# Laying all operands of one-pass matrix products at one residue modulo 512 bytes in a hybrid decoder layer

## The chip, the core and the metric

The kernel runs on one core of one Trainium2 chip. The metric is the device time of one launch in microseconds (us); three runs of the kernel before took 1207.21, 1209.97 and 1210.71 us, median 1209.97 us. Five engines work side by side: TensorE (PE in the rows; its weight loads are PEld), VectorE (DVE), ScalarE (ACT), GpSimd (POOL) and SyncE (SP, which here only issues transfers).

## What is computed

One decoder layer over 512 tokens of 1024 features, in float32. A mixing sublayer projects the normed input once into all branches, runs four of them, and merges them under gates; a gated MLP follows.

```python
def mixing_sublayer(h, mem_n, w_in, ...):
    z = h @ w_in
    xa, ga, q, k, v, us, xq, gates = jnp.split(z, SPLIT_IDX, axis=-1)
    ya = rg_lru_branch(xa, ga, ...)
    yb = dilated_attention(q, k, v)
    yc = s5_branch(us, ...)
    yx = memory_cross_attention(xq, mem_n, mem_wkv)
    g = jax.nn.sigmoid(gates.reshape(B_, L, N_BRANCH, D_MODEL))
    m = (g[:, :, 0] * (ya @ proj_a) + g[:, :, 1] * (yb @ proj_b)
         + g[:, :, 2] * (yc @ proj_c) + g[:, :, 3] * (yx @ proj_x))
    return m @ w_out

def conv_gated_mlp(h, w_up, conv_w, conv_b, w_down):
    up = h @ w_up
    val = up[..., :D_FF]
    gate = causal_dwconv(up[..., D_FF:], conv_w, conv_b)
    return (val * jax.nn.gelu(gate)) @ w_down

def reference(x, mem, ...):
    h = rms_norm(x, g_mix_pre); mem_n = rms_norm(mem, g_mem)
    x = x + rms_norm(mixing_sublayer(h, mem_n, ...), g_mix_post)
    h = rms_norm(x, g_mlp_pre)
    return x + rms_norm(conv_gated_mlp(h, ...), g_mlp_post)
```

## The kernel before

**Products.** A float32 product is made of three one-pass products. Each operand is split into a high part, rounded to the type `float32r` of one pass, and a low part, the rest: `split` (line 94) and `wload` (line 75) do it with a copy on ACT and a subtraction on DVE. Then low·high, high·high and high·low are summed in PSUM; `mm3` (line 83) is the loop for a stored unit of weights. In each product one operand is loaded into the array first (the stationary one, 128 columns of 4 bytes, which are 512 bytes of a partition) and the other streams past it (the moving one, 512 or 256 columns of 4 bytes). In a row such as `up<-h2l,whi` the moving operand stands first and the stationary one second: the activations `h2l` move past the weights `whi`, while in `dn<-whi,aTh` and `wo<-woh,mm0h` the weights move past the activations.

**Weights.** A unit of weights is [128, 1024] float32 (512 KB). `wfetch` (line 70) brings it in on SP's queue, three buffers deep, and `wload` splits it into `whi` and `wlo`, three buffers each. One unit is enough for 24 products of 512 columns.

**Order of the work.** Python writes the instructions in order, and each engine runs its own in that order. The stages are: norms and the memory's keys and values; RG-LRU; memory cross-attention; S5 with the gates of two branches between its steps; dilated attention, twice two heads of each group, with the GLU of S5 and the third branch's gates between; the gates and products with `yb` (`merge(1, yb, 2, ...)`, lines 667 and 669); `w_out` with the residual and the norm (lines 680 to 795); the upward products of the MLP (`up`, line 775, and `upu`, line 808), whose results go through the convolution and GELU on ACT and DVE and are split into `aT` (line 829); the downward products (`down`, line 833); and the last norm.

**Places in SBUF.** Tiles come from pools that lie one behind another, and one side of the memory is filled from the right. The size of each tile fixes the place of the next, so a tile's distance from a multiple of 512 bytes is left to what lies before it. In the built program the weights `whi` and `wlo`, the normed input `hT`, the memory's `mT`, and the branch results `ya`, `yx`, `yc` and the GLU's input `gy`, the merged `mm0` and `mm1`, and `woh` and `wol` all lie at 384 modulo 512; the other operands of one-pass products lie elsewhere (the table in the section on the change).

**Lines that the change touches.** Line 181 (`vx`, the memory's values, in the pool on the right before `xq`), line 451 (`sel0`, a table of 2x128 numbers that is copied to `selr` and used by `combine`, line 596), line 479 (`nmc`, the negated maxima of the attention's rows), line 679 (`cols`, sums of squares, between `h2` and the next tiles of the pool on the right), line 788 (`we`, the fourth unit of upward weights), and line 803 (`fcb`, a bias of the convolution, ahead of `aT`).

The loops that the steps speak of:

```python
def up(b, w, cs, ks=range(KC)):                      # line 775
    for k in ks:
        sl = slice(k * 128, (k + 1) * 128)
        for n, (a, x) in enumerate(((w[0], h2[1]), (w[0], h2[0]), (w[1], h2[0]))):
            PE.matmul(b[:, cs], a[:, sl], x[:, k, cs], ...)

def down(t, nh, k, w):                               # line 833
    for n, (a, b) in enumerate(((0, w[1]), (0, w[0]), (1, w[0]))):
        PE.matmul(acc[t, nh], aT[a][:, k, ts_], b[:, cs], ...)
```

Of the kernel before, what the change touches and what calls it, by code (L numbers as in the profile page):

```python
# [12 lines left out]
F32 = mybir.dt.float32  # L13
F32R = mybir.dt.float32r
# [4 lines left out]
PSUM = bass.MemoryType.PSUM  # L19
# [31 lines left out]
def _body(ctx, tc, nc, D):  # L51
# [31 lines left out]
    def mm3(out, w, x, nk):  # L83
        """out[128, N] = sum over nk chunks of w_k^T x_k, operands given as exact hi + lo parts."""
        whi, wlo = w
        n = 0
        for k in range(nk):
            sl = slice(k * 128, (k + 1) * 128)
            for a, b in ((whi, 1), (whi, 0), (wlo, 0)):
                last = PE.matmul(out, a[:, sl], x[b][:, k], start=(n == 0), stop=(n == 3 * nk - 1))  # L90
                n += 1
        return last

    def split(hi, lo, src, scale=None, eng=V):
        """hi + lo = src (* scale), hi rounded to the width of one pass."""
        if scale is None:
            a = S.copy(hi, src)
            b = eng.tensor_tensor(out=lo, in0=src, in1=f32(hi), op=ALU.subtract)  # L98
        else:
            a = S.activation(hi, src, AF.Identity, scale=scale)  # L100
            b = V.scalar_tensor_tensor(out=lo, in0=src, scalar=scale, in1=f32(hi), op0=ALU.mult, op1=ALU.subtract)
        return a, b
# [11 lines left out]
    def rstd_of(pool, s0, s1, n, tag, bufs=1, between=None, eng=V):  # L114
        """((s0 + s1) / DM + EPS) ** -0.5, with a Newton step after the table's root; between() goes beside the root."""
        t, y, e, r = (pool.tile([128, n], F32, tag=tag + x, name=tag + x, bufs=bufs) for x in "tyer")
        if s1 is None:
            eng.tensor_scalar(out=t, in0=s0, scalar1=EPS * DM, scalar2=None, op0=ALU.add)
        else:
            eng.tensor_scalar(out=t, in0=s0, scalar1=s1, scalar2=EPS * DM, op0=ALU.add, op1=ALU.add)  # L120
        S.activation(y, t, AF.Sqrt, scale=1.0 / DM)
        if between is not None:
            between()
        V.reciprocal(y, y)
        if n == 1:
            eng.tensor_scalar(out=e, in0=y, scalar1=y, scalar2=t, op0=ALU.mult, op1=ALU.mult)
        else:
            eng.tensor_tensor(out=e, in0=y, in1=y, op=ALU.mult)
            eng.tensor_tensor(out=e, in0=e, in1=t, op=ALU.mult)
        eng.tensor_scalar(out=e, in0=e, scalar1=-0.5 / DM, scalar2=1.5, op0=ALU.mult, op1=ALU.add)  # L130
        eng.tensor_tensor(out=r, in0=y, in1=e, op=ALU.mult)
        return r
# [28 lines left out]
    def turned_rows(xs, gain, dst, k0, k1):  # L161
        """dst[k] (hi, lo) <- xs turned to have features on partitions, times gain."""
        for k in range(k0, k1):
            b = axb("nT")
            for t in range(4):
                PE.transpose(b[:, t * 128:(t + 1) * 128], xs[t][:, k * 128:(k + 1) * 128], ident)
            last = split(dst[0][:, k, :], dst[1][:, k, :], b, scale=gain[:, k:k + 1])
        return last

    mp = ctx.enter_context(pool("mp"))  # L170
    # the memory's keys of a head's whole chunks (0 .. 3) and, with the other head's rows at zero, shared ones (4 .. 7)
# [9 lines left out]
    vx = tuple(kvp.tile([128, 2, 768], F32R, name="vx" + s) for s in "hl")  # L181
# [13 lines left out]
    with pool("np") as npool:  # L195
# [9 lines left out]
        # the rows' scale comes after the products  # L205
# [80 lines left out]
    ya = ynew("ya")  # L286
    with pool("lru", bufs=2) as lp, pool("lruc") as lc:
# [5 lines left out]
        with tc.issue_after(normed[0].ins), tc.issue_after(normed[1].ins):  # L293
            for b in (ba, bx):
                V.tensor_scalar(out=b, in0=b, scalar1=0.5, scalar2=None, op0=ALU.mult)
            # softplus(-lam) = max(-lam, 0) + log1p(e), e = exp(-|lam|), by the series of 2 atanh(e / (2 + e))
            V.scalar_tensor_tensor(out=ab, in0=lam, scalar=-1.0, in1=lam, op0=ALU.mult, op1=ALU.max)
            S.activation(e, ab, AF.Exp, scale=-1.0)
            V.tensor_scalar(out=s, in0=e, scalar1=2.0, scalar2=None, op0=ALU.add)
            V.reciprocal(s, s)  # L300
            V.tensor_tensor(out=s, in0=s, in1=e, op=ALU.mult)
            V.tensor_tensor(out=s2, in0=s, in1=s, op=ALU.mult)
            V.memset(q, 1.0 / 17)
            for d in (15, 13, 11, 9, 7, 5, 3, 1):
                V.tensor_tensor(out=q, in0=q, in1=s2, op=ALU.mult)
                V.tensor_scalar(out=q, in0=q, scalar1=1.0 / d, scalar2=None, op0=ALU.add)
            V.tensor_tensor(out=q, in0=q, in1=s, op=ALU.mult)
            V.tensor_scalar(out=ab, in0=lam, scalar1=-1.0, scalar2=0.0, op0=ALU.mult, op1=ALU.max)
            V.scalar_tensor_tensor(out=q, in0=q, scalar=2.0, in1=ab, op0=ALU.mult, op1=ALU.add)
            V.tensor_scalar(out=chf, in0=q, scalar1=4.0, scalar2=None, op0=ALU.mult)  # L310
            V.tensor_scalar(out=nch, in0=q, scalar1=-4.0, scalar2=None, op0=ALU.mult)
# [137 lines left out]
    apx = ExitStack()  # L449
    ap = apx.enter_context(pool("at"))  # L450
    sel0 = ap.tile([2, 128], F32, name="selh")
# [4 lines left out]
    # order of the tokens in a group: 4 tiles of 128  # L456
# [12 lines left out]
    class Attention:  # L469
        """Two heads of each group."""  # L470

        def __init__(self, h2):
            self.h2 = h2
            self.ab = []
            for g, w in enumerate((256, 128, 128)):
                t = ap.tile([128, 2, w], F32, tag="ab%d" % g, name="ab%d" % g)
                nc.gpsimd.dma_start(out=t, in_=D["ab%d" % g][:, 2 * h2:2 * h2 + 2, :])
                self.ab.append(t)
            self.nmc = ap.tile([128, 3, 4, 2], F32, tag="nmc", name="nmc")
            # maxima in columns 0 and 1, sums in 32 and 33  # L480
            self.col = ap.tile([128, 3, 4, 34], F32, tag="col", name="col")
            G.memset(self.col, 0.0)
            self.mcol, self.lcol = self.col[:, :, :, 0:2], self.col[:, :, :, 32:34]
            self.q, self.k, self.v, self.o, self.segs, self.vT = {}, {}, {}, {}, {}, {}
# [16 lines left out]
        def units_k(self, g):  # L501
            b = unit(U_K + 2 * g + self.h2, "k")
            # each head's keys, the other head's rows at zero
# [63 lines left out]
        def weigh(self):  # L567
            # weights of the groups, per head and token: exp(m_g - M) / sum_g exp(m_g - M) l_g
# [40 lines left out]
        def run(self, fill, before=None):  # L609
            """The group's steps between products that don't wait for them; before() comes with the first."""  # L610
# [68 lines left out]
    cols = x1p.tile([128, 16], F32, name="cols")  # L679
    with pool("wo") as wo:  # L680
# [93 lines left out]
        # the first products of the MLP in halves of the tokens, the first of which are there sooner  # L774
# [13 lines left out]
        w = tuple(x1p.tile([128, 1024], F32R, name="we" + s) for s in "hl")  # L788
# [14 lines left out]
    fcb = fp.tile([128, 24], F32, name="fcb")  # L803
# [40 lines left out]
    # the last products by tiles of tokens, whose weights stand where h2 did  # L844
# [32 lines left out]
def s5_params(nc, tc, D, keep_pool, pool):  # L877
    V, S = nc.vector, nc.scalar
    r = {}
    with pool("s5t") as tp:  # L880
# [29 lines left out]
        def exp(o, x):  # L910
            """exp(x) = 2^n exp(r): the power of two from the table, rid of its error by its mantissa's bits, times a polynomial."""
# [31 lines left out]
        # z = (A - 1) / lambda  # L943
# [26 lines left out]
        # powers of A  # L970
# [8 lines left out]
        # a chunk's decay, and the powers 0 .. 15 and 0, 16 .. 112 of its rotation  # L979
# [25 lines left out]
class S5:  # L1005
    """S5 in batches of eight groups (four pairs) over 128 chunks of 4 tokens: lanes are (group of the pair, state)."""
# [12 lines left out]
    def tables(self, i):  # L1019
        """The rotations R^c of the chunks, and V_j = A^(3 - j) B."""  # L1020
# [33 lines left out]
    def prepare(self, i):  # L1054
        """The batch's matrices: inputs to chunk sums, states to outputs, inputs to outputs within a chunk."""
# [7 lines left out]
        # inputs: [(j, group of the pair, h), pair, chunk]  # L1063
# [3 lines left out]
        # W_n = C A^n  # L1067
# [14 lines left out]
        # K_tau = Re(C A^tau B), tau = 0 .. 3, with D on its first diagonal  # L1082
# [55 lines left out]
    def states(self, i):  # L1138
        """The batch's states before each chunk."""
# [7 lines left out]
        # sums of a chunk's inputs, turned back by its rotation  # L1147
# [19 lines left out]
        # states before each chunk  # L1167
# [12 lines left out]
    def outputs(self, i):  # L1180
        """GELU of the batch's outputs, chunks on partitions."""
        S, PE, st = self.nc.scalar, self.nc.tensor, self.b[i]
        U, (xr, xi) = st["U"], st["x"]
        # y: [chunk, pair, (group, j, h)]
# [9 lines left out]
    def turned(self, i):  # L1194
        """The same with features on partitions, tokens in (j, c) order, in a bank of PSUM."""
# [70 lines left out]
```

## Time and profile before

| | |
|---|---|
| three runs | 1207.21, 1209.97, 1210.71 us |
| median | 1209.97 us |
| profiled execution | span of the one core 1209.4 us (first to last instruction); no other time of it is on record |
| PE | 1181.5 us busy, 98% of the span, 5778 products |
| PEld | 970.7 us |
| DVE | 685.4 us |
| ACT | 516.8 us |
| POOL | 132.4 us |
| moved by DMA | 119.16 MB, mean 99 GB/s |

The span is the time from the first to the last instruction on the core; the median of the runs is 0.6 us longer. Products are pipelined: each row of a product lasts some 390 ns from its start to its modelled end, and the next one starts long before that end. So the pace of TensorE is not read from the mean of one product but from a stretch of the chain: its length divided by the number of products in it. The chain is the sequence of work that ended last, followed back from the last instruction.

### The profile page before, as it was taken

What the parts mean: (1) busy time and instruction counts of PE and PEld (TensorE: products, weight loads), DVE (VectorE), ACT (ScalarE), POOL (GpSimd) and SP (SyncE); (2) the same over time, 40 slices, a digit from 0 to 9 for tenths busy, and PEclk for the clock granted to TensorE, in tenths of its full rate; (3) what the DMA queues carried; (4) which work ended last, traced back from release to release, by engine and by line L of the source; (5) the groups of instructions that cost most, each with busy time, mean ns of one, the idle gap of its engine ahead of it and who ended that gap; (6) DMA issues with size and microseconds to landing.
All of it is one profiled execution on the core that took longest, in us unless ns stands there. A gap on an engine that the chain in (4) does not pass through costs nothing.

```text
span 1209.4 us, 15139 instructions
## 1 busy us (share of the span) xinstructions
PE 1181.5 (98%) x5778; PEld 970.7 (80%) x5778; DVE 685.4 (57%) x1246; ACT 516.8 (43%) x871; POOL 132.4 (11%) x172
## 2 busy tenths in 40 slices
PE   7999999999999999999999999999999999999997
PEld 7877788877787887878888888888888888888886
DVE  5756795688797634485447455475445444432224
ACT  5669833553334235443533233455343443421122
POOL 3200100096561000000000000010000000000000
PEclk9999999999999999999999999999999999999999
DMA  6432252122323322213122324613322223223221
GB/s 244 166 105 70 92 180 76 31 83 78 92 76 100 112 90 66 84 62 122 62 79 75 92 92 134 236 37 105 104 89 91 102 87 103 90 89 102 88 87 69
DMA packets 43720, 119.16 MB, mean 99 GB/s; under 512 B 9566, under 2 KB 13744, under 8 KB 43648
## 3 DMA queue, kind: packets, MB, share of 16 engines
q1 hardware_dynamic: 42000, 114.69, 28.6%
q0 software_dynamic: 1072, 2.46, 0.7%
q8 instruction: 45, 0.74, 0.2%
q10 hardware_dynamic: 576, 1.05, 0.2%
q14 instruction: 27, 0.22, 0.1%
HBM read 114.17 MB, written 4.01 MB: 98 GB/s over the span
## 4 chain that ended last, share of the span: by engine, by line
PE 82%; DVE 9%; ACT 4%; DMA 2%; POOL 1%; issue 1%; SPq 0%; DVEq 0%; ACTq 0%; POOLq 0%
PE up L779 22%; PE gate L90 13%; PE dn L837 11%; PE prj L90 7%; PE v L90 3%; PE k L90 3%; PE q L90 3%; PE us L90 3%; PE xq L90 3%; PE glu L90 2%; PE ga L90 2%; DVE wlo L80 1%; PE kv L90 1%; PE kv L257 1%; PE xs L378 1%
## 5 line engine op out<-in xcount | busy, mean ns | idle before, releaser
L80 DVE TENSOR_TENSOR wlo<-wraw,whi 128x1024 fp32r<-128x1024 f32 (+1 forms) x198 | 230.5, 1166 | 290.4 <-ACT whi L79 282.0
L79 ACT CAST whi<-wraw 128x1024 fp32r<-128x1024 f32 (+1 forms) x198 | 194.3, 984 | 455.3 <-PE up L779 110.7
L779 PE MATMUL up<-h2l,whi 128*128 128x512 f32 (+1 forms) x400 | 152.7, 382 | 1.0 <-DVE h2l L98 1.0
L779 PE MATMUL up<-h2h,whi 128*128 128x512 f32 (+1 forms) x400 | 152.6, 381 | 0.0
L779 PE MATMUL up<-h2h,wlo 128*128 128x512 f32 (+1 forms) x400 | 152.5, 381 | 0.0
L90 PE MATMUL gate<-hTl,whi 128*128 128x512 f32 x256 | 101.2, 395 | 0.0
L90 PE MATMUL gate<-hTh,whi 128*128 128x512 f32 x256 | 100.2, 392 | 0.0
L90 PE MATMUL gate<-hTh,wlo 128*128 128x512 f32 x256 | 100.0, 391 | 0.0
L779 PEld LDWEIGHTS up<-h2l,whi 128*128 128x128 f32 x400 | 75.1, 188 | 17.6 <-DVE h2l L98 1.5
L779 PEld LDWEIGHTS up<-h2h,whi 128*128 128x128 f32 x400 | 75.1, 188 | 16.2
L779 PEld LDWEIGHTS up<-h2h,wlo 128*128 128x128 f32 x400 | 75.1, 188 | 16.0
L837 PE MATMUL dn<-whi,aTh 128*128 128x512 f32 x160 | 63.2, 395 | 0.0
L837 PE MATMUL dn<-whi,aTl 128*128 128x512 f32 x160 | 63.2, 395 | 0.0
L837 PE MATMUL dn<-wlo,aTh 128*128 128x512 f32 x160 | 63.2, 395 | 0.0
L90 PEld LDWEIGHTS gate<-hTl,whi 128*128 128x128 f32 x256 | 48.1, 188 | 10.1 <-issue 0.5
L90 PEld LDWEIGHTS gate<-hTh,wlo 128*128 128x128 f32 x256 | 48.1, 188 | 10.0 <-DVE wlo L80 0.2
L90 PEld LDWEIGHTS gate<-hTh,whi 128*128 128x128 f32 x256 | 48.1, 188 | 9.5
L828 DVE TENSOR_TENSOR fc<-fc,up 128x512 f32<-128x512 f32 x24 | 16.5, 689 | 44.8 <-PE up L779 43.5
L825 DVE SCALAR_TENSOR_TENSOR fc<-gs,fcw,fc 128x512 f32<-128x512 f32 x48 | 36.1, 751 | 0.8
L837 PEld LDWEIGHTS dn<-wlo,aTh 128*128 128x128 f32 x160 | 30.0, 188 | 7.3
L837 PEld LDWEIGHTS dn<-whi,aTh 128*128 128x128 f32 x160 | 30.0, 188 | 7.3
L837 PEld LDWEIGHTS dn<-whi,aTl 128*128 128x128 f32 x160 | 30.0, 188 | 7.3
(520 smaller groups left out, 2566.3 us busy)
## 6 DMA issues: line engine op xcount, KB each, us to landing
wraw<-w_in SPq DMA_DIRECT2D x74, 512.0 KB, 3.5
wraw<-ffn_w_up SPq DMA_DIRECT2D x48, 512.0 KB, 3.5
wraw<-ffn_w_down SPq DMA_DIRECT2D x24, 512.0 KB, 3.4
wraw<-proj SPq DMA_DIRECT2D x24, 384.0 KB, 3.0
wraw<-ssm_glu SPq DMA_DIRECT2D x12, 384.0 KB, 2.9
wraw<-w_out SPq DMA_DIRECT2D x8, 512.0 KB, 4.2
wraw<-mem_wk SPq DMA_DIRECT2D x6, 512.0 KB, 6.5
wraw<-mem_wv SPq DMA_DIRECT2D x6, 512.0 KB, 3.4
```

Source lines behind the costliest of these rows:

```text
L79: S.copy(hi[:, :n], raw[:, :n])
L80: V.tensor_tensor(out=lo[:, :n], in0=raw[:, :n], in1=f32(hi[:, :n]), op=ALU.subtract)
L90: last = PE.matmul(out, a[:, sl], x[b][:, k], start=(n == 0), stop=(n == 3 * nk - 1))
L257: done = PE.matmul(bv[t][:, :256], mT[a][:, 4 * kh + k, t * 128:(t + 1) * 128], w[:, cs], start=(kh == 0 and k == 0 and o == 0), stop=(kh ...
L378: PE.matmul(b[:, j * 256:(j + 1) * 256], xq[:, x, ch, t * 128:(t + 1) * 128], kx[:, y, i], start=(n == 0 and o == 0), stop=(n == 1 and o = ...
L779: PE.matmul(b[:, cs], a[:, sl], x[:, k, cs], start=(k == 0 and n == 0), stop=(k == KC - 1 and n == 2))
L825: V.scalar_tensor_tensor(out=c, in0=gs[:, j:j + 512], scalar=fcw[:, i, j:j + 1], in1=c, op0=ALU.mult, op1=ALU.add)
L828: V.tensor_tensor(out=c, in0=c, in1=bv, op=ALU.mult)
L837: PE.matmul(acc[t, nh], aT[a][:, k, ts_], b[:, cs], start=(k == 0 and n == 0), stop=(k == 23 and n == 2))
```

## The change

Six tiles get another size or another place, so that the tiles behind them move. No instruction is added or taken out.

```diff
@@ the memory's values
-    vx = tuple(kvp.tile([128, 2, 768], F32R, name="vx" + s) for s in "hl")
+    vx = tuple(kvp.tile([128, n], F32R, name="vx" + s)[:, :1536].rearrange("p (k c) -> p k c", k=2) for s, n in (("h", 1536), ("l", 1560)))
...
@@ dilated attention
-    sel0 = ap.tile([2, 128], F32, name="selh")
+    sel0 = t2("selh")[0:2, :128]
...
-            self.nmc = ap.tile([128, 3, 4, 2], F32, tag="nmc", name="nmc")
+            self.nmc = ap.tile([128, 104], F32, tag="nmc", name="nmc")[:, :24].rearrange("p (g t h) -> p g t h", g=3, t=4)
...
@@ w_out, residual
-    cols = x1p.tile([128, 16], F32, name="cols")
+    cols = x1p.tile([128, 128], F32, name="cols")
...
-        w = tuple(x1p.tile([128, 1024], F32R, name="we" + s) for s in "hl")
+        w = tuple(x1p.tile([128, n], F32R, name="we" + s)[:, :1024] for s, n in (("h", 1024), ("l", 1048)))
...
@@ conv-gated MLP
-    fcb = fp.tile([128, 24], F32, name="fcb")
+    fcb = fp.tile([128, 56], F32, name="fcb")[:, :24]
```

The rest of the diff takes out comments and docstrings. The places that follow from it in the two built programs, as residues modulo 512 bytes of the tile's start (a step from one chunk of 128 or 512 columns to the next is a multiple of 512 bytes, so the residue is that of each product):

| one-pass products | number, columns | moving before, after | stationary before, after |
|---|---|---|---|
| `up<-h2`, with `whi`, `wlo` | 1056 of 512; 144 of 256 | 416, 384 | 384, 384 |
| `up<-h2`, with `weh`, `wel` | 48 of 256 | 416, 384 | 480, 384 |
| `dn<-aT`, with `whi`, `wlo` | 480 of 512 | 384, 384 | 256, 384 |
| `dn<-aT`, with `wlh`, `wll` | 96 of 512 | 416, 384 | 256, 384 |
| `prj<-yb` | 48 of 512 | 64, 384 | 384, 384 |
| `xo<-vx` | 48 of 512 | 384, 384 | 480, 384 |
| `xs<-kx,xq` | 96 of 256 | 384, 384 | 480, 384 |
| `bc<-wr,selr` | 12 of 512, two rows | 64, 384 | 384, 384 |
| `sc<-k,q` (attention's scores) | 18 of 512; 54 of 256 | 64, 384 | 64, 384 |
| all others (`gate`, `prj<-ya`, `prj<-yx`, `prj<-yc`, `glu`, `wo`, `kv`, and the other units of `w_in`) | | 384, 384 | 384, 384 |

Products in plain float32 (transposes, S5, the values of the attention) are not padded for; some of their tiles move along with the rest.

`sel0` now comes from the pool of six work tiles `t2` and no longer from the attention's own pool. Its transfer and the copy that reads it stand at other places. On POOL, which issues the transfer, at the start of dilated attention (`ab` are the tables of biases, `col` the columns of maxima and sums):

```order
-L452 DMA selh<-selh 2x128
 L477 DMA ab_4147<-ab 128x512
 L477 DMA ab_4149<-ab 128x256
 L477 DMA ab_4151<-ab 128x256
 L482 MEMSET col 128x408
+L452 DMA selh<-selh 2x128
 L477 DMA ab_5075<-ab 128x512
```

The transfer of `selh` moved behind the first three tables and the clearing of `col`. On ACT, in the last step of S5, where the copy stands (`gl` is the GELU of S5's outputs, `th` the gate of a merge, `whi` the high parts of the next weights):

```order
 L1192 ACTIVATE gl<-y_4054 128x512
+L79 CAST whi<-wraw 128x1024
+L273 ACTIVATE th<-gate 128x512
 L454 CAST selr<-selh 2x128
-L79 CAST whi<-wraw 128x1024
-L273 ACTIVATE th<-gate 128x512
 L79 CAST whi<-wraw 128x1024
```

The copy moved behind one unit of weights and one gate. On PE, DVE and SP the order is the same in both programs.

## Rows read from the trace of the kernel before

**Rows 1.** The page: the span, PE's busy time, the granted clock in 40 slices.
```profile
span 1209.4 us, 15139 instructions
PE 1181.5 (98%) x5778; PEld 970.7 (80%) x5778; DVE 685.4 (57%) x1246; ACT 516.8 (43%) x871; POOL 132.4 (11%) x172
PEclk9999999999999999999999999999999999999999
```

**Rows 2.** Chain that ended last, in order of time (start us, length us, what), the MLP.
```profile
806.46 1.72 PE up L779 x15
...
809.05 258.84 PE up L779 x1161
1067.89 134.50 PE dn L837 x576
```

**Rows 3.** The same chain, gates and products with `yb`, one after another.
```profile
693.34 5.71 PE gate L90 x24
...
705.91 1.40 PE prj L90 x6
707.31 5.46 PE gate L90 x24
712.77 1.40 PE prj L90 x6
714.17 5.46 PE gate L90 x24
```

**Rows 4.** The same chain, products of 256 columns, and the units of `xq`.
```profile
45.44 11.51 PE kv L257 x96
...
166.73 32.64 PE xq L90 x144
...
223.05 2.85 PE xs L378 x24
...
320.35 5.49 PE gate L90 x24
```

**Rows 5.** Groups on PE with shapes apart (count; busy us, mean ns).
```profile
L779 PE MATMUL up<-h2l,whi 128*128 128x512 f32 x352 | 139.1, 395 | 0.0
L837 PE MATMUL dn<-whi,aTh 128*128 128x512 f32 x160 | 63.2, 395 | 0.0
L699 PE MATMUL wo<-woh,mm0h 128*128 128x512 f32 x40 | 15.6, 389 | 0.0
L837 PE MATMUL dn<-wll,aTh 128*128 128x512 f32 x32 | 12.7, 397 | 0.0
L405 PE MATMUL xo<-xpTh,vxh 128*128 128x512 f32 x16 | 6.3, 396 | 0.0
```

**Rows 6.** Busy time by stretch: PE, PEld, DVE, ACT, POOL, clock, DMA share, GB/s.
```profile
600.00:700.00 100.00, 100.00 (x483) 82.08 (x482) 55.14 (x85) 35.40 (x70) 0.00 (x0) 1.00 0.24 77
1000.00:1100.00 100.00, 100.00 (x430) 80.42 (x430) 39.90 (x48) 33.63 (x43) 0.00 (x0) 1.00 0.28 91
```

**Rows 7.** POOL and DVE in order of time, the end of S5.
```profile
388.18 0.55 POOL L452 DMA_DIRECT2D selh<-selh  x1 [21.90 <-DVE z L1062]
...
395.12 0.46 POOL L482 MEMSET col<- 128x408 f32 x1
...
393.44 0.69 DVE L281 TENSOR_TENSOR m<-m,th 128x512 f32<-128x512 f32 x1
```

**Rows 8.** ACT in order of time, 420.75 to 431 us.
```profile
421.24 0.28 ACT L454 CAST selr<-selh 2x128 fp32r<-2x128 f32 x1
426.01 1.05 ACT L79 CAST whi<-wraw 128x1024 fp32r<-128x1024 f32 x1 [4.49 <-PE gate L90]
426.96 0.59 ACT L273 ACTIVATE th<-gate 128x512 f32<-128x512 f32 x1
430.09 1.05 ACT L79 CAST whi<-wraw 128x1024 fp32r<-128x1024 f32 x1 [2.54 <-PE prj L90]
```

**Rows 9.** The tile `selh`: time of its transfer from issue to landing.
```profile
DMA to landing us min/median/max: 2.8/2.8/2.8
```

## The prediction

> **What bounds the kernel.** The page comes first: PE is busy for 98% of the span and no other engine for more than 57%, and the granted clock is nine tenths or more in every slice [rows 1]. Then the chain that ended last: the upward products of the MLP are one unbroken piece of 258.84 us and the downward ones another of 134.50 us, up to the last norm [rows 2]. In a stretch like that no wait ends last; the time is the number of products times the distance from one start to the next. So I read that distance, stage by stage, as length over count.
>
> Downward: 134.50 us / 576 = 233.5 ns [rows 2]. Upward: of the 1248 products of line 779, 192 have 256 columns; 72 of them (three units) and 15 more [rows 2] come earlier, so 105 lie in the long piece. At 119 ns each (below) they take 12.5 us, and (258.84 - 12.5) us / 1056 = 233.3 ns. Elsewhere it is less: the units of `xq` take 32.64 us / 144 = 226.7 ns [rows 4], a unit of gates 5.46 us / 24 = 227.5 ns [rows 3]. All have operands of the same shape and type, and the granted clock is 1.00 in such stretches [rows 6]. The clearest rows are those in which the two kinds alternate: between two units of gates stand six products with `yb`, 1.40 us / 6 = 233.3 ns, then gates again at 227.5 [rows 3]. Both are issued by line 90 and both have `whi` and `wlo` as the stationary operand; what differs is the tile that moves past: `hT` lies at 384 modulo 512 like the weights, `yb` at 64.
>
> The means of single products say the same more coarsely [rows 5]: 395 to 397 ns where the residues differ (`up`, `dn` with either place of its weights, `xo`), 389 where they agree (`wo`). `wo` is the fair partner of `dn`, since in both the weights move and the activations stand. The unequal pairs have four different distances, on either side, and all run at the slower pace; so equality is what counts in these rows, not one lucky residue.
>
> **The change, part by part.** New pace: the bounds are 226.7 ns (`xq`) and 228.8 ns (the gate unit at 320 us, 5.49 us / 24 [rows 4]). I take 227.5, the gates of [rows 3], since their stretch is the nearest in what goes on beside it: DVE 55 and ACT 35 us in 100 there, 40 and 34 in the MLP [rows 6].
>
> - Upward, 1056 of 512 columns: 233.3 - 227.5 = 5.8 ns each, 6.1 us (ends: 4.5 ns, 4.8 us; 6.6 ns, 7.0 us).
> - Downward, 576: 6.0 ns each, 3.5 us (ends 2.7 and 3.9 us). This piece has PE alone on the chain until the last norm, so all of it counts.
> - `prj<-yb`, 48: 5.8 ns, 0.3 us (0.2 to 0.3). They too stand in the chain.
> - `xo<-vx`, 48: the same price would be 0.3 us, but in that stage the chain changes hands often; I take half, 0.15 us (0 to 0.3).
> - Products of 256 columns: here equal residues are not the faster ones. `kv`, equal: 11.51 us / 96 = 119.9 ns. `xs`, unequal: 2.85 us / 24 = 118.8 ns [rows 4]. The fourth upward unit, unequal: 1.72 us / 15 = 114.7 ns [rows 2]. So 48 products lose 5.2 ns (0.25 us), and 144 upward and 96 `xs` lose 1.1 ns each (0.25 us): together 0.5 us lost. Ends: 288 x 5.2 ns = 1.5 us lost, or half of what 512 columns gain, 288 x 2.9 ns = 0.8 us won.
> - The scores' tiles are at equal residues before and after, and `bc` has 12 products: nothing.
> - Plain float32 products whose tiles move: no pair becomes equal by design, and I put them at nothing; they are short and mostly stand between waits.
>
> **The moved step.** `selh` takes one of six work tiles. The tile it replaces is a gate's `th`, read for the last time by the addition that ends at 393.44 + 0.69 = 394.1 us; the transfer is issued behind the clearing of `col`, which ends at 395.6 us, and lands 2.8 us later, near 398.4 us [rows 7, 9]. Its reader on ACT now comes behind the gate that ends at 427.6 us [rows 8], some 29 us later: it waits for nothing. The copy takes 0.28 us and falls into the 2.54 us in which ACT is idle ahead of the next weights at 430.09 us [rows 8]. On POOL only the tables for the second half of attention stand behind the transfer. Cost: nothing. If that cover were gone, every microsecond of lateness would hold the next `whi`, and 2.5 us later PE.
>
> **Does something else become the bound?** A unit of 24 products shrinks from 5.60 to 5.46 us. Gates run at that pace with the same 512 KB and the same two splits to a unit, and DVE has 60 us in 100 free in the MLP [rows 6]. The weights' transfers need 24 products' time for 512 KB, 96 GB/s where 91 flow now. No.
>
> Sum: 6.1 + 3.5 + 0.3 + 0.15 - 0.5 = 9.6 us off the profiled span of 1209.4 us [rows 1], 1199.8 us; the median of the runs is 0.6 us over that span, so the time is **1200.4 us**. Ends: 4.8 + 2.7 + 0.2 - 1.5 = 6.2 us off, 1203.8 us; 7.0 + 3.9 + 0.3 + 0.3 + 0.8 = 12.3 us off, 1197.7 us.
>
> **A rule that speaks against it.** In these rows the pace goes with the pair of places of the moving and the stationary operand [rows 3, 5]. The Trainium skill, "TensorE: Matmul & The Clock Gate", section "Step-by-step: what each phase is for", says that TensorE has two independent read ports into SBUF and that loading the next weights takes no read bandwidth from the running product. By that the places could not matter, nothing would be won, and the sum would be zero; the trace does not agree, with 233.3 against 227.5 ns in one stage.
>
> **The rivals.**
>
> 1. *The place is a coincidence: no change.* The MLP and the few products with `yb` could be slower for another reason, for instance how much ACT and DVE write beside them. Then `up` and `dn` stay at 233.3 and 233.5 ns and the time is 1210.0 us. For it: no run has yet moved one tile alone. Against it: the alternation in [rows 3], where both kinds have the same neighbours, and the MLP, where DVE is less busy than beside the gates [rows 6] and yet the pace is slower. The rule above would also end here. Chance 0.07.
> 2. *Only one of the two MLP stages gains.* Moving and stationary operand change roles between them. If `dn` stayed, 3.5 us less are won: 1203.9 us; if `up` stayed, 6.1 us less: 1206.5 us, which is no change. Against: `wo` has the roles of `dn`, the gates those of `up`, and both have the short means. Chance 0.05, four fifths of it with `dn`.
> 3. *Slower.* Once everything lies at one residue, the writes of the splits on ACT and DVE into `aT`, `whi` and `wlo` fall on the residue that PE reads twice, and PE waits for them. Place: the MLP. Price: the slowest equal unit in the rows, 5.71 us / 24 = 237.9 ns [rows 3]; 4.6 ns x 1056 + 4.4 ns x 576 + 0.5 us = 7.9 us more, 1217.9 us. It decides from a pace above the 233.3 ns of today. Against: the gates that follow, with the same splits beside them, are back at 227.5, so that unit's excess is more like a single wait at its start. Chance 0.02.
>
> **How the numbers follow.** The forecast has 0.86. A measurement of this kernel can tell about 0.3% from no change, 3.6 us; faster is below 1206.3 us, slower above 1213.6. Faster: 0.86 + 0.04 = 0.90. Same: 0.01 + 0.07 = 0.08. Slower: 0.02. The range: the ends of the sum, 1197.7 and 1203.8, widened by the scatter of the runs, which goes 2.8 us below the median and 0.7 above: 1195.5 to 1204.5 us. This takes in the case that `dn` alone stays; the rest, 0.10, is left out, with a little for a sum whose terms miss together.
>
> **What would show it.** In the profile after, the piece `up` x1161 of the chain should take some 253 us (1056 x 227.5 ns and 105 at 120) instead of 258.84, the piece `dn` x576 some 131.0 instead of 134.50; six products with `yb` 1.37 us instead of 1.40; means near 390 ns in the groups of `up` and `dn`; `kv`, gates and `xq` as before. The start of the upward stage should stand within 1 us of where it stands now. The prediction is wrong if `up` or `dn` keeps 233 ns, if ACT shows a wait ahead of `selr`, or if PE gets idle time in the MLP ahead of weights that are not split yet.

## The result and the profile after

The changed kernel took 1195.57 us (median of four runs, 1194.35 to 1198.25) against 1208.59 us before (four runs, 1206.82 to 1210.71): a ratio of 0.9895, 95% interval 0.9876 to 0.9915. A second comparison, further down, gave 0.991 (0.9885 to 0.9936). Between the medians the kernel is 13.0 us faster in the first comparison and 10.2 us in the second; the forecast was 9.6 us off, 1200.4 us.

The page of the profiled execution (its own time is 1194.35 us), with the rows that answer to [rows 1]:

```profile
span 1192.5 us, 15140 instructions
PE 1164.5 (98%) x5778; PEld 966.2 (81%) x5778; DVE 684.4 (57%) x1246; ACT 516.7 (43%) x871; POOL 133.4 (11%) x172
```

PE has the same products and 17 us less of busy time; DVE, ACT and POOL are as busy as before within 1 us. The chain that ended last (start us, length us, what), for [rows 2 to 4]:

```profile
14.68 15.71 PE kv L90 x131
...
42.08 11.52 PE kv L257 x96
...
163.42 32.64 PE xq L90 x144
...
219.69 2.87 PE xs L378 x24
...
700.06 1.36 PE prj L90 x6
701.42 5.44 PE gate L90 x24
...
790.43 8.89 PE up L779 x72
...
800.19 1.79 PE up L779 x15
...
802.85 252.13 PE up L779 x1161
1054.99 130.57 PE dn L837 x576
```

The two MLP pieces went from 258.84 to 252.13 us and from 134.50 to 130.57 us: 6.71 and 3.93 us, 10.6 together. Per product that is 130.57 / 576 = 226.7 ns downward, and (252.13 - 105 x 0.120) / 1056 = 226.8 ns upward, the pace that `xq` had all along and still has (32.64 us for 144). The six products with `yb` take 1.36 us instead of 1.40, 226.7 ns. The groups of single products say the same [rows 5]; `wo`, which the change does not touch, stands for comparison:

```profile
L779 PE MATMUL up<-h2l,whi 128*128 128x512 f32 x352 | 136.9, 389 | 0.0
L837 PE MATMUL dn<-whi,aTh 128*128 128x512 f32 x160 | 62.2, 389 | 0.0
L699 PE MATMUL wo<-woh,mm0h 128*128 128x512 f32 x40 | 15.6, 389 | 0.0
L837 PE MATMUL dn<-wll,aTh 128*128 128x512 f32 x32 | 12.4, 389 | 0.0
```

In `up` and `dn` 395 to 397 ns became 389, exactly that of `wo`; in `xo`, which has waits between, 396 became 393 (`xo<-xpTh,vxh`). The moved step, on POOL and ACT [rows 7, 8]:

```profile
390.21 0.53 POOL L452 DMA_DIRECT2D selh<-selh  x1
...
421.65 0.59 ACT L273 ACTIVATE th<-gate 128x512 f32<-128x512 f32 x1
422.14 0.28 ACT L454 CAST selr<-selh 2x128 fp32r<-2x128 f32 x1
424.78 1.05 ACT L79 CAST whi<-wraw 128x1024 fp32r<-128x1024 f32 x1 [2.36 <-PE prj L90]
```

The transfer is issued some 32 us ahead of the copy, the copy comes right behind the gate with no idle time ahead of it, and ACT is still idle for 2.36 us (2.54 before) ahead of the next weights: it cost nothing.

The spans differ by 16.9 us, 6.3 us more than the two pieces explain: the MLP's first products start at 790.43 us, where they started at 796.83 us before. Three rows of the chain of the kernel before, for this and for what follows:

```profile
15.95 17.75 PE kv L90 x131
...
672.71 5.44 PE gate L90 x24
...
796.83 8.76 PE up L779 x72
```

Half of this lead is there before any moved tile is used: the last 131 products of the memory's keys end at 30.39 us (14.68 + 15.71) instead of 33.70, and the values (`kv` of line 257) start at 42.08 us instead of 45.44. What differs there is the clock. Between 14.5 and 17.5 us (PE, PEld, DVE, ACT, POOL, then the granted clock; first the kernel before, then the changed one, then the run `half256` of the experiments):

```profile
14.50:17.50 3.00, 2.78 (x11) 2.60 (x12) 1.71 (x3) 2.29 (x5) 0.17 (x1) 1.00 0.96 381
14.50:17.50 3.00, 3.00 (x26) 2.98 (x25) 1.67 (x3) 2.72 (x7) 0.00 (x0) 1.00 1.01 396
14.50:17.50 3.00, 3.00 (x14) 2.82 (x14) 1.23 (x1) 2.29 (x5) 0.00 (x0) 0.50 1.02 396
```

In the third row the granted clock is 0.50, the lower of its two levels (1.2 instead of 2.4 GHz), and the products of 256 columns start 213 ns apart. In the kernel before they start 213 ns apart too, up to 20.0 us, and 120 ns apart from then on; in the changed kernel they are at 120 ns from 11.1 us on. The 1.00 of the first row is no measurement, since the record of the clock in that trace begins only at 20.0 us, with the full clock (in the changed kernel's at 8.9 us). In the first 10 us PE had been busy for 3.65 us in the kernel before and for 4.15 us in the changed one. Thirty products at 213 instead of 120 ns are 2.8 of the 3.3 us.

Between 305 and 325 us the clock differs again (first the kernel before, then the changed one):

```profile
305.00:325.00 20.00, 17.79 (x112) 15.47 (x111) 13.35 (x23) 8.29 (x19) 11.96 (x16) 0.91 0.32 89
305.00:325.00 20.00, 17.67 (x117) 15.06 (x116) 14.88 (x28) 8.60 (x19) 9.48 (x13) 1.00 0.33 89
```

A mean granted clock of 0.91 is a part of the stretch at 1.2 instead of 2.4 GHz; over 20 us that is at most 1.8 us of clock that the changed kernel got in this execution and the kernel before did not, in the stage of S5 where PE waits now and then. Whether these two parts are the change's or chance is the question of one run below.

### The profile page after: what moved, and what is told of

Its sections match the earlier page's. It is cut to its first block, busy times and chain, and to the rows that moved or that the text cites. A ratio compares the mean times of both kernels' runs of the same rounds, so it can differ in the third digit from the quotient of the medians.

```text
span 1192.5 us, 15140 instructions
## 1 busy us (share of the span) xinstructions
PE 1164.5 (98%) x5778; PEld 966.2 (81%) x5778; DVE 684.4 (57%) x1246; ACT 516.7 (43%) x871; POOL 133.4 (11%) x172
## 4 chain that ended last, share of the span: by engine, by line
PE 84%; DVE 7%; ACT 4%; DMA 2%; POOL 2%; issue 1%; SPq 0%; DVEq 0%; ACTq 0%; POOLq 0%
PE up L779 22%; PE gate L90 14%; PE dn L837 11%; PE prj L90 8%; PE v L90 3%; PE k L90 3%; PE q L90 3%; PE us L90 3%; PE xq L90 3%; PE glu L90 2%; PE ga L90 2%; PE kv L90 1%; DVE wlo L80 1%; PE kv L257 1%; PE xs L378 1%
```

## The experiments

The theory ahead of them: a product of 512 columns takes 226.7 ns when its moving and its stationary operand lie at the same residue, and 233.4 when they do not, whatever else goes on. Eight kernels ran: seven edits of the changed kernel, and the changed kernel itself once more. The first six ran once each, and single times of one kernel lie up to 7 us apart (1204.22 to 1211.23 us in seven runs of the kernel before). So they are read by the pieces of the chain, which come out the same to 0.01 us where nothing in them was changed.

### Distances in steps of 64 bytes

```diff
-    h2 = tuple(x1p.tile([128, KC, L], F32R, tag="h2" + s, name="h2" + s) for s in "hl")
+    h2 = tuple(x1p.tile([128, KC, L + 16], F32R, tag="h2" + s, name="h2" + s)[:, :, :L] for s in "hl")
...
-    aT = tuple(fp.tile([128, 24, L], F32R, name="aT" + s) for s in "hl")
+    aT = tuple(fp.tile([128, 24, L + 16], F32R, name="aT" + s)[:, :, :L] for s in "hl")
...
```

> The changed kernel with 16 columns (64 bytes) more between one chunk and the next of h2 and of aT, so that chunk k lies 64 k bytes on, modulo 512; the weights stay at 384. Equality theory: only the chunk at 384 is fast. up: 132 products at 227.0 ns, 924 at 233.4, 105 of 256 columns at 118: the long piece takes 258.0 us (changed kernel 252.1). dn: 72 products at 226.7, 504 at 233.4: 134.0 us (130.6). Every other chunk reads 233 to 234 ns whatever its distance. Rival, distance: the pace goes with the size of the distance, and some distance other than 0 reads below 227 ns, down to the 114.7 ns of 256 columns doubled, so that a better place than equality exists. Rival, high places: the place is without effect and the gain came from something else; then both pieces stay at 252.1 and 130.6 us.

Measured, 1206.21 us; the chain:

```profile
807.20 257.20 PE up L779 x1161
1064.40 133.06 PE dn L837 x576
```

Both pieces are slow again, by 5.1 and 2.5 us, and each is about 0.9 us better than strict equality would have it. Where that comes from is seen by taking the mean distance from one start to the next, from the rows of single products, for each place of the chunk (ns; stationary minus moving for `dn` with `whi` and `wlo`, moving minus stationary for `up`):

```
bytes      0      64     128    192    256    320    384    448
dn       228.5  233.1  232.2  229.6  228.3  233.1  232.2  229.7
up       230.0  232.9  232.2  231.7  230.0  232.8  232.2  231.7
```

The columns repeat after 256 bytes. The place matters, so the third theory is out, and no distance here is faster than equality, which was the second; but the first is not right either, since 256 bytes apart is as good as equal. The means of one place are not settled ones, since in `up` the place changes after every three products and in `dn` after twelve.

### Distances in steps of 16 and of 4 bytes

```diff
+    h2 = tuple(x1p.tile([128, KC * (L + 4) + 96], F32R, tag="h2" + s, name="h2" + s)[:, :KC * (L + 4)].rearrange("p (k n) -> p k n", k=KC)[:, :, :L] for s in "hl")
...
+    aT = tuple(fp.tile([128, 24 * (L + 1) + 104], F32R, name="aT" + s)[:, :24 * (L + 1)].rearrange("p (k n) -> p k n", k=24)[:, :, :L] for s in "hl")
...
```

> The changed kernel with 16 bytes more from chunk to chunk of h2 (distances 0, 16, ... 112 bytes) and 4 bytes more from chunk to chunk of aT (0, 4, ... 92 bytes), both parts of an operand alike. Equality theory, strict: only distance 0 is fast; up piece 258.2 us, dn piece 134.2 us. Equality by granule: places count in lines of 16, 32 or 64 bytes, and all distances inside one line are fast: with 64 bytes half of the up chunks and 16 of 24 dn chunks are fast, 255.3 and 131.9 us. Distance theory: the pace rises step by step from 227 to 233.5 ns over the chunks instead of jumping.

Measured, 1204.96 us:

```profile
804.83 257.43 PE up L779 x1161
1062.25 133.93 PE dn L837 x576
```

The pieces are nearest to strict equality (258.2 and 134.2 us) and far from lines of 64 bytes (255.3 and 131.9). But this run settles little on small distances: with the place moving on after three products, even the chunk of `h2` at distance 0 reads 232.7 ns, so neighbours in time matter and not only the pair of one product.

### All tiles from the left at 0 instead of 384

```diff
+    first = cp.tile([128, 32], F32, name="first")
+    V.memset(first, 0.0)
     ident = cp.tile([128, 128], F32, name="ident")
```

> The changed kernel with one tile of 128 bytes at the bottom of the memory, so that every tile that is filled from the left moves from 384 to 0 modulo 512, while those filled from the right (vx, xq, h2, wl, we) stay at 384. Equality theory: gates (0, 0) keep 5.44 us for 24, dn keeps 227 ns for 480 products and pays for 96 with wl: 131.2 us, up is unequal again (384, 0): 258.7 us; time 7 us above the changed kernel. Rival, 384 is a lucky residue: gates and all units of the first part read 233 ns, 5.60 us for 24, dn 134.5 us, and the time is some 25 us above the changed kernel (2664 products of 512 columns outside the MLP at 6.5 ns, and 11 us).

Measured, 1200.96 us:

```profile
715.75 5.44 PE gate L90 x24
...
802.94 258.05 PE up L781 x1161
1060.98 131.26 PE dn L839 x576
```

Gates at 0 and 0 take the same 5.44 us as at 384 and 384, `dn` pays for its last 96 products only, and `up`, whose `h2` stayed at 384, is back near its old pace ((258.05 - 12.5) / 1056 = 232.5 ns). So 384 is not a lucky residue. For the upward piece this run is at the same time the changed kernel without its part for `up`: that part is worth 5.9 us in place (258.05 - 252.13).

### One of three stationary tiles 32 bytes off

```diff
-    aT = tuple(fp.tile([128, 24, L], F32R, name="aT" + s) for s in "hl")
+    aT = tuple(fp.tile([128, 24 * L + n], F32R, name="aT" + s)[:, :24 * L].rearrange("p (k c) -> p k c", k=24) for s, n in (("h", 8), ("l", 0)))
```

> The changed kernel with 32 bytes between aTh and aTl: aTh lies at 384 like the weights, aTl at 416. The order of dn is (aTh, wlo), (aTh, whi), (aTl, whi). If the pair of one product decides: the 192 products with aTl take 233.4 ns and the other 384 take 227, dn piece 131.8 us. If the operand that is loaded while a product runs decides (the next product's stationary one): it is the 192 products dn<-whi,aTh that take 233.4 ns, the same 131.8 us in all. If both must fit: 384 of 576 are slow, 133.1 us. up and gates as in the changed kernel in each case.

The 8 columns more behind `aTh` put `aTl` at 416. Measured, 1200.63 us, with the chain and the starts of two products with `aTl`, three products apart:

```profile
805.33 252.13 PE up L779 x1161
1057.46 134.41 PE dn L837 x576
```

```profile
1099.76 0.39 PE L837 MATMUL dn<-whi,aTl 128*128 128x512 f32 x1
...
1100.46 0.39 PE L837 MATMUL dn<-whi,aTl 128*128 128x512 f32 x1
```

All three expectations failed. The downward piece is as slow as before the change, 233.3 ns on the mean, though two of three products have equal operands. The single distances were 228.0 ns from the start of a product with `aTl`, 233.0 with `aTh` and `wlo`, 239.0 with `aTh` and `whi`: 700 ns for three, which is three times 233.3. The distances are the same throughout the piece. One tile out of step takes the whole gain from the loop that it is in; the upward piece, which it is not in, stays at 252.13 us.

### Each distance held for 48 products

```diff
+    STEP = [0, 2, 4, 8, 16, 24, 32, 40, 48, 64, 64, 64]
...
+    def chunk(s, k):
+        o = k * L + STEP[k // 2]
+        return aTf[s][:, o:o + L]
...
```

> The changed kernel with the stationary operand aT moved away from 384 by a distance that stays the same for two chunks (24 products in a row, twice): 0, 8, 16, 32, 64, 96, 128, 160, 192 and 256 bytes for the first ten pairs of chunks, 256 for the last eight chunks (with wl). After the runs before, where chunks at 0 and 256 bytes read alike, three theories. Period 512: only distance 0 settles at 226.7 ns, all others at 233 to 234, dn piece 133.9 us. Period 256: 0 and 256 settle at 226.7, all others at 233 to 234, dn piece some 132.8 us. Graded: the pace grows with the distance up to 128 and falls again, 64 bytes near 230.

`STEP` counts columns of 4 bytes, one entry for two chunks. Measured, 1198.25 us. The first product of each distance, in order of time (start us, length us), and the whole piece from the chain:

```profile
1056.49 0.39 PE L842 MATMUL dn<-wlo,aTh 128*128 128x512 f32 x1
1067.37 0.40 PE L842 MATMUL dn<-wlo,aTh 128*128 128x512 f32 x1
1078.45 0.39 PE L842 MATMUL dn<-wlo,aTh 128*128 128x512 f32 x1
1089.65 0.40 PE L842 MATMUL dn<-wlo,aTh 128*128 128x512 f32 x1
1100.84 0.40 PE L842 MATMUL dn<-wlo,aTh 128*128 128x512 f32 x1
1112.05 0.39 PE L842 MATMUL dn<-wlo,aTh 128*128 128x512 f32 x1
1123.28 0.39 PE L842 MATMUL dn<-wlo,aTh 128*128 128x512 f32 x1
1134.44 0.40 PE L842 MATMUL dn<-wlo,aTh 128*128 128x512 f32 x1
1145.64 0.40 PE L842 MATMUL dn<-wlo,aTh 128*128 128x512 f32 x1
1156.64 0.40 PE L842 MATMUL dn<-wlo,aTh 128*128 128x512 f32 x1
...
1056.65 132.82 PE dn L842 x576
```

Each difference of two starts, divided by 48, is the pace at one distance: 226.7 ns at 0; 230.8 at 8 bytes; 233.3 at 16; 233.1 at 32; 233.5 at 64; 234.0 at 96; 232.5 at 128; 233.3 at 160; 229.2 at 192. At 256 bytes the first four distances from start to start are 236, 228, 233 and 231 ns, and from the fifth product on they are 226 or 227, to the end of the piece. That is the second theory, down to the 132.8 us of the piece, with two in-between values, at 8 and at 192 bytes, that no theory had.

### The change at 256 bytes instead of 512

```diff
-    cols = x1p.tile([128, 128], F32, name="cols")
+    cols = x1p.tile([128, 192], F32, name="cols")
...
-    fcb = fp.tile([128, 56], F32, name="fcb")[:, :24]
+    fcb = fp.tile([128, 120], F32, name="fcb")[:, :24]
```

> The changed kernel with h2 (and wl) and aT 256 bytes further, at 128 modulo 512, while the weights stay at 384: the two sides of up and dn differ by 256 bytes, but agree modulo 256. Period 512: both pieces are slow again, up 258.7 us, dn 133.8 us (the last 96 products are equal). Period 256: both stay as in the changed kernel, up 252.1 us, dn 130.6 us.

Measured, 1197.09 us:

```profile
805.63 252.13 PE up L779 x1161
1057.76 130.57 PE dn L837 x576
```

To the last digit the pieces of the changed kernel, with every operand pair of `up` and 480 of the 576 of `dn` 256 bytes apart modulo 512. What has to agree is the residue modulo 256 bytes; the theory of a period of 512 bytes is out.

### The changed kernel once more

No edit, to see what of the 6.3 us ahead of the MLP comes back.

> The changed kernel once more, unchanged. If the time before the MLP differed in the first comparison (MLP 6.3 us earlier, of which 3.3 us within the first 32 us) by chance of the start and of the clock, this profile has the same two MLP pieces, 252.1 and 130.6 us, but reaches the 150th product anywhere from 28.8 to 32.1 us after the start, and the time is 11 to 13 us below the kernel before over many runs. If the shift is the change's, it is at 28.8 us again.

Measured, 1197.41 us (four runs, 1195.68 to 1198.23; before 1207.63 us over seven runs, 1204.22 to 1211.23), ratio 0.991 (0.9885 to 0.9936). The chain of its profile:

```profile
15.77 17.77 PE kv L90 x131
...
45.26 11.51 PE kv L257 x96
...
794.26 8.90 PE up L779 x72
...
806.70 252.13 PE up L779 x1161
1058.83 130.57 PE dn L837 x576
```

The MLP pieces are the same two numbers. The early start is gone: the values of the memory begin at 45.26 us, where the kernel before had 45.44 and the first profile of the changed one 42.08. The 131 products of the keys took 17.77 us here, 17.75 us before and 15.71 us in the first profile, and the reason is the clock once more: here, too, products start 213 ns apart up to 20.3 us. So the 3.3 us at the start belong to the execution and not to the change. From the values of line 257 to the first upward product it is 751.4 us before (796.83 - 45.44), and 748.4 and 749.0 in the two profiles after. Both of the latter have one low stretch of the clock in S5 where the kernel before has two (granted clock from 270 to 290 us 0.91 before, then 0.91 and 1.00; from 305 to 325 us 0.91 before, then 1.00 and 0.91), worth 1.8 us at most. That leaves about 1 us ahead of the MLP; `prj<-yb` explains 0.3 us of it and `xo` perhaps 0.2, and no run here separates the rest from scatter.

### Narrow products 64 bytes apart

```diff
+        shift = npool.tile([128, 16], F32, name="shift")
...
-    xq = xqp.tile([128, 2, 6, 512], F32R, name="xq")
+    xq = xqp.tile([128, 6256], F32R, name="xq")[:, :6144].rearrange("p (s i t) -> p s i t", s=2, i=6)
```

> The changed kernel with the operands of 256-column products in the first part set 64 bytes apart: mT at 448 against weights at 384, xq at 448 against kx at 384; before the change products of 256 columns with 64 bytes between them took 114.7 ns, equal ones 119.9. Theory, narrow products want 64 bytes: xs takes 24 x 114.5 = 2.75 us for 24 (2.88 now), the 96 values of the memory 11.0 us (11.5), in all 288 + 96 products at 5 ns = 1.9 us less than after_again at most. Rival, the fourth upward unit was short for another reason (its place at the start of a wait): all stay at 117 to 120 ns and the time is that of after_again.

`shift` moves `mT` to 448, and the longer tile moves `xq` to 448. Measured, 1197.21 us (four runs, 1195.7 to 1198.52), ratio 0.9913 (0.9891 to 0.9934):

```profile
44.16 10.91 PE kv L259 x96
...
221.14 2.83 PE xs L380 x24
```

The values of the memory went from 11.51 to 10.91 us, 113.6 ns each, as the theory had it. The scores of cross-attention went only from 2.87 to 2.83 us, and the memory's keys, 144 products with the same `mT` on line 90, from 119.9 to 117.8 ns each. So products of 256 columns can run faster unequal than equal, but 64 bytes do not give the same in every loop, and the 0.6 us cannot be seen in the time, which is that of the run before within its scatter. No kernel here beats the changed one by more than the measurement can tell.

## Why the prediction was right, and where it was off

- **What bounds the kernel.** Right: PE's pace in the two dense pieces sets their length, and what comes behind them did not grow (7.0 us to the end of the span, before and after).
- **Equal residues give the pace of the gates.** Right in its effect, and shown by taking the parts apart: `up` goes back to 258.05 us when its pair is unequal, all residues at 0 are as good as at 384, and `dn` walks from 226.7 to 233 ns and back as its tile is moved. As it was put it was too strict in one way and too loose in another. Too strict: 256 bytes apart is equal. Too loose: it is not a matter of the pair in one product alone, since one tile of three off its place makes the three together as slow as three unequal ones.
- **The size of the gain.** The term that was mis-sized is the new pace. I took 227.5 ns, from the gates, because their neighbours were the nearest; measured were 226.8 and 226.7, the bound from `xq`. That made the MLP 10.6 us instead of 9.6. The gates' extra 0.8 ns came with the place after all: gates between products with equal places took 5.44 us in the kernel before already (672.71 above), and only those behind six products with `yb` took 5.46, because their first five distances from start to start are 226, 236, 228, 232 and 231 ns and the others 225 to 228. With `yb` at their residue they take 5.44 too.
- **The time.** As a difference, the 10.2 us of the second comparison lie inside the ends of the sum (6.2 and 12.3 us off), and the 13.0 us of the first lie outside. In the profiled executions of the first, the changed kernel had the full clock 11 us earlier at the start and one low stretch less in S5, some 5 us together, which no term had. How much of the medians this makes is not shown, since one execution of each kernel has a trace there. The range itself was added up wrongly at its lower end: 1197.7 less the 2.8 us of scatter is 1194.9, not 1195.5. That 1195.57 us lies inside the stated range is luck by 0.07 us. And the 0.6 us of the median over the span compared different executions: wherever both numbers of a run are on record, its time is 1.7 to 1.9 us longer than its span. This moves nothing, since the forecast is the median less 9.6 us, but it says that the profiled execution of the kernel before was a slow one.
- **The start of the upward stage.** One sign on the list failed: the stage should have started within 1 us of its old place, and it started 6.4 us earlier in the first profile and 2.6 us earlier in the second (794.26 us). The clock makes some 5 us of the first and at most 1.8 us of the second. The prediction took the clock for full in every slice from the page [rows 1], and that trace has no record of it in the first 20 us.
- **The narrow products.** Right in sign and near in size: the first 72 upward products of 256 columns went from 8.76 to 8.89 us, the fifteen of the fourth unit from 1.72 to 1.79, `xs` from 2.85 to 2.87 for 24.
- **The moved step.** Right: no wait, no idle time.
- **The rivals.** "The place is a coincidence" fell with the result and with every run that moved a tile. "Only one stage gains" fell: both did. "Slower, by writes to the same residue" fell: the MLP has all its tiles at one residue and runs at 226.7 to 226.8 ns, the pace of `xq`. The rule of the Trainium skill in "TensorE: Matmul & The Clock Gate", section "Step-by-step: what each phase is for", that loading the next weights takes no read bandwidth in SBUF from the running product, is no guide to the pace here: in `dn_steps` it is 226.7 or 233.3 ns by the place of the stationary tile alone, at the full granted clock and with the same instructions.

What stays open is the mechanism inside: that the reads of the two operands get in each other's way when their places differ would be a guess, since no run shows the reads. Why 192 bytes on one side lie between fast and slow (229.2 ns), while 64 bytes are slow (233.5), was not tried further.

## What to carry to other kernels

When a dense stretch of weight load and product runs at two different paces in one kernel, compare the places of the operands before looking for waits: here tiles whose starts agree modulo 256 bytes, moving and stationary alike, run one-pass products of 512 columns 3% faster, and some 1.1 KB of padding to a partition, in five places, is all it cost. All tiles of the inner loop must take part, because one out of step takes the gain from its neighbours too; and products of half the width need not follow, so read their rows apart. Before a difference ahead of the changed stretch is put down to the change, compare the clock at the start, and where the profile has no record of it, the pace of the first products.

## What the runs showed of the hardware

- The pace of one-pass products of 512 columns depends on the distance between the places of the two operands with a period of 256 bytes: 226.7 ns at 0 and at 256, 232.5 to 234.0 from 16 to 160 bytes, 229.2 at 192, 230.8 at 8.
- It depends on the products just before: after a change of distance from 192 to 256 bytes the first four starts are 236, 228, 233 and 231 ns apart and the following ones 226 or 227, gates behind six products with `yb` have the same (236, 228, 232, 231 after a first 226), and a cycle of three products with one tile 32 bytes off takes 700 ns, as much as three wholly unequal ones, split as 228, 233 and 239.
- Products of 256 columns take 119.9 ns equal and 113.6 ns with 64 bytes between them in the loop of line 257, so there the order of better and worse turns round with the width; with 64 bytes between them the keys on line 90 take 117.8 ns and `xs` 117.9.
- In two executions of the same kernel products of 256 columns started 120 ns apart from 11.1 us on, or 213 ns apart up to 20.3 us and 120 ns from then on, and the last 131 products of the memory's keys took 15.71 or 17.77 us: some 3 us of a comparison of two single profiles can come from the clock at the start alone.
